# Moving a skipped overflow pass and the last weight loads around it, at the end of a two-layer mixture-of-experts kernel

## Chip, core and metric

The kernel runs on one core of a Trainium2 chip. The metric is device time in microseconds (us), the median of three runs of the whole kernel.

## The reference

Two layers on 256 latent and 256 context tokens of width 1024. Each has a mixer (a gated linear recurrence and pooling in layer 0, two kinds of attention in layer 1) and a mixture of experts: 4 groups of 8 experts, of which each token takes 2. In layer 1 only the latent tokens go on to the output, which is normalised. The part that the change touches is the mixture of experts of layer 1:

```python
def hier_moe(h, w_rg, b_rg, w_re, b_re, w_gate, w_up, w_down):
    ...
    comb = (g_p[:, :, None] * jax.nn.one_hot(g_idx[:, 0], MOE_GROUPS, dtype=jnp.float32)[:, :, None]
            * e_w[:, None, :]).astype(h.dtype)
    y = jnp.zeros_like(x)
    for g in range(MOE_GROUPS):
        a = jax.nn.silu(jnp.einsum('td,edf->tef', x, w_gate[g])) * jnp.einsum('td,edf->tef', x, w_up[g])
        y = y + jnp.einsum('tef,efd->td', a * comb[:, g, :, None], w_down[g])
    return y.reshape(b_, n, d)
...
    return rmsnorm(x, final_norm_g)
```

## The kernel before

The 32 experts of a layer are worked off in 8 quads of 4. Each expert has 32 slots (CAP), so a quad fills the 128 rows of a tile. For quad q the steps are, with the tiles that the profile names:

- `gather` picks the tokens of the quad with matmuls (xg) and evacuates them as X, 4 of 8 chunks on ACT and 4 on DVE.
- `gate_up` multiplies X by the gate and up weights (tiles g and u, 1 MB for each expert; 64 matmuls for each of the two), then makes sge.
- `turned` transposes sge to aT. `selection` builds the matrix sc that scatters the result: a broadcast matmul (bc) of rqT, the ranks of all tokens, which `rank_rows` makes with matmuls (rqT) and a cast on ACT.
- `down` multiplies aT by the down weights (tile d, 1 MB for each expert) to y, and `scatter` adds sc times z to x. For the last two quads the sums stay in PSUM (xo).

The steps of neighbouring quads overlap: in turn q of the loop in `moe` stand gate/up of q, scatter of q-2, down of q-1 and the gather for q+1. A scheduler orders the instructions of each engine when the program is built, except those that `keep` holds in program order.

Weights are loaded by SP, in the order of the program, into tiles from a ring of buffers (`wm`). Eight semaphores, DMAHW0 to DMAHW7, are used in turn, so that a load waits for the one eight before it. fg, the final gain (0.5 MB, one row spread over all partitions), is one such load.

An expert with more than 32 tokens is served by `overfull`: a branch on the largest count (`cmx`), and inside it loops over the quads that overflow. With these inputs the pass of layer 1 is skipped. Each engine loads the count into a register and branches for itself. The program of either side must leave the semaphores with the same counts: the not-taken side has, for each engine, waits until its own semaphores show all that was issued before, and adds what the pass would have added. For DMAHW0 to DMAHW7 SP does this, one after the other. `rank_rows` follows the branch, since the pass overwrites rqT.

Of the kernel before, what the change touches and what calls it, by code (L numbers as in the profile page):

```python
# [6 lines left out]
F32 = mybir.dt.float32  # L7
# [8 lines left out]
P = 128  # L16
D = 1024
# [55 lines left out]
def drain(*gens):  # L73
    for g in gens:
        for _ in g:
            pass
# [16 lines left out]
class K:  # L93
# [1312 lines left out]
    def moe(self, layer):  # L1406
        nc = self.nc
        V = nc.vector
        cap, nt, nq, S = self.CAP, self.nt, self.NQ4, self.S
        self.py = self.open(f"moey{layer}", side="right")  # L1410
        self.px = self.open(f"moex{layer}", side="right")
        self.p = p = self.open(f"moe{layer}", side="right")
        nr, nx, ny = self.RING, self.nx, self.YRING[layer]
        head = self.slots
        first = [(self.cst, "x0", 1)] + [(self.mla, f"s{i}", 1) for i in (1, 2, 0)] + [(self.yr, "yr", self.NYR)] * self.NYR if layer else []
        late = [(self.outer, "mh", 1), (self.outer, "ml", 1)] if layer else []
        rings = [[(self.ring, "w", nr)] * (nr - len(head)), [(self.xring, "xw", nx)] * nx]
        self.slots = head + first + rings[self.RO[layer]] + rings[1 - self.RO[layer]] + late + [(self.px if layer else self.py, "yw", ny - 1)] * (ny - 1) + [(self.px, "yl", 1)]
        self.prefetch(len(self.slots) - len(head) - 1)
        segs = list(range(S))  # L1420
        if layer:
            cmx = self.counts()
            drain(self.gather(self.rv, 0, 4, 0, self.X))
        if S > 1:
            self.gate2(0, 1, p, nc.gpsimd)

        def more(rv, q):
            self.rank_rows(rv)
            for s in segs:
                X = {}  # L1430
                if not layer:
                    self.over = self.px.tile([P, 2, 1024], F32, name="over", tag="yl")
                drain(self.gather(rv, 4 * q, 4, s, X, over=True))
                st = self.quad(q, X, [s], self.load_one)
                self.gate_up(st)
                self.turned(st)
                self.down(st, [s])
                self.scatter(st, [s])

        def overfull():  # L1440
            cnt = nc.values_load(cmx[0:1, nq:nq + 1], min_val=0, max_val=2 * P)
            with self.tc.If(cnt > cap):  # L1442
                rv2 = p.tile([P, nt, 32], F32, name="rv2")
                V.tensor_copy(rv2, self.rv)
                for q in range(nq):
                    es = slice(4 * q, 4 * q + 4)
                    cg = nc.values_load(cmx[0:1, q:q + 1], min_val=0, max_val=2 * P)
                    with self.tc.For_i(cap, cg, cap):
                        V.tensor_scalar_add(rv2[:, :, es], rv2[:, :, es], -float(cap))
                        more(rv2, q)  # L1450

        cur = self.quad(0, self.X, segs, self.load)
        if layer:
            self.gate_up(cur)
        else:
            self.low(0)
            self.gate_up(cur, 0, self.ranks)
            cmx = self.counts()
            drain(self.gather(self.rv, 0, 8, 1, self.X, low=self.low))
            overfull()  # L1460
            cur["X"] = dict(self.X)
            self.gate_up(cur, 1)
        self.prefetch(1)
        self.rank_rows(self.rv)
        Q = {}
        for q in range(nq):
            end = q == nq - 1
            if layer and end:
                self.scatter(Q[q - 2], segs)
                pre = {(key, 4 * q + j): self.load(key, 4 * q + j) for key in "gu" for j in range(4)}  # L1470
                Q[q - 1]["d"] = {j: self.load("d", 4 * q - 4 + j) for j in range(4)}
                dl = {j: self.load("d", 4 * q + j) for j in range(4)}
                self.pre.update(pre)
                self.fg = self.wm("fg")[:, :D]
                fg = self.I["final_norm_g"]
                nc.sync.dma_start(self.fg, bass.AP(tensor=fg.tensor, offset=fg.offset, ap=[[0, P], [1, D]]))
                self.over = self.xring.tile([P, 2, 1024], F32, name="over", tag="xw", bufs=self.nx)
                overfull()
                self.rank_rows(self.rv)
                self.keep = True  # L1480
                Q[q - 1]["into"] = True
            if cur is None:
                cur = self.quad(q, self.X, segs[::-1] if end else segs, self.load)
                self.gate_up(cur)
            if layer and end:
                cur["d"] = dl
            Q[q], cur = cur, None
            if S > 1 and q % 2 and not end:
                for s in segs:
                    drain(self.gather(self.rv, 4 * q + 4, 8, s, self.X))  # L1490
            if q > 1 and not (layer and end):
                self.scatter(Q[q - 2], segs)
            if layer and end:
                Q[q - 1]["py"] = {(0, hf): self.ps("y") for hf in range(2)}
                self.xo = {(n, hf): self.ps("xo") for hf in range(2) for n in range(2)}
                for n, hf in self.xo:
                    self.mmk(self.xo[n, hf], self.ident, self.xi(2 + n)[:, hf * 512:hf * 512 + 512], start=True, stop=False)
                self.selection(Q[q - 1])
            if q:
                self.down(Q[q - 1], segs)  # L1500
            self.turned(Q[q])
            if S == 1 and not end:
                drain(self.gather(self.rv, 4 * q + 4, 4, 0, self.X))
        self.scatter(Q[nq - 2], segs[::-1])
        for s in segs[::-1]:
            self.down(Q[nq - 1], [s])
            self.scatter(Q[nq - 1], [s])
        if layer:
            self.final()
        self.p.release()  # L1510
        self.px.release()
        self.py.release()
        self.mp.release()
        if layer:
            self.yr.release()
            self.outer.release()
            self.close_xring()
            self.mla.release()
# [9 lines left out]
    def load(self, key, e, *_):  # L1528
        return self.pre.pop((key, e), None) or self.fetch(self.wm(f"{key}_{self.layer}_{e}"), key, e)
# [234 lines left out]
    def down(self, st, segs):  # L1764
        nc, p, I = self.nc, self.p, self.I
        V, S, A = nc.vector, nc.scalar, nc.tensor
        q, parts, load, last = st["q"], st["parts"], st["load"], st["last"]
        py = st.get("py") or {(s, hf): self.ps("y") for s in segs for hf in range(2)}
        step = 1 if parts == 2 else 4
        kn = 2 // parts  # L1770
        for h in range(0, 4, step):
            for k0 in range(0, 2, kn):
                if parts == 2:
                    ws = {h: load("d", 4 * q + h, k0, k0 + kn)}
                else:
                    ws = st["d"] = st.get("d") or {j: load("d", 4 * q + j) for j in range(4)}
                for s in segs:
                    for hf in range(2):
                        for k in range(k0, k0 + kn):
                            for j, w in ws.items():  # L1780
                                r = slice(32 * j, 32 * j + 32)
                                first = not (h or k0 or hf or k or j or s != segs[0])
                                (self.mmy if parts == 1 and not self.layer and not first else self.mmk)(py[s, hf][r, :], st["aT"][s][:, k, r], w[:, k - k0, hf * 512:(hf + 1) * 512], start=k == 0, stop=k == 1)
        if last:
            zz = self.wm("z", F32R)
            self.yg = self.wm("yg")
# [61 lines left out]
```

## Time and profile before

| | |
|---|---|
| timed runs, median of 3 | 1088.25 us (1087.97 to 1088.27) |
| profiled execution, timed | 1088.17 us |
| its span in the profile | 1085.4 us |
| mean granted TensorE clock | 0.96 of full |
| busy: TensorE, VectorE, ScalarE, GpSimd | 89%, 49%, 37%, 22% of the span |
| read from HBM | 293.5 MB |

The span runs from the first to the last instruction of the profile; 2.8 us of the timed execution lie outside it. TensorE counts as busy from a matmul's start to its modelled end. PE is TensorE, PEld its weight loads, DVE is VectorE, ACT is ScalarE, POOL is GpSimd; a q behind a name is the engine's sequencer, which also waits, branches and issues DMAs. Line numbers are those of the kernel before; in the changed kernel the lines behind the edit in `moe` are 6 higher.

### The profile page before, as it was taken

The numbers are of one execution on the slowest core, as the hardware profiler recorded it, in microseconds if no ns is written. First come the engines' busy times: TensorE is split into PE (matmuls) and PEld (weight loads), VectorE is DVE, ScalarE is ACT, GpSimd is POOL, SyncE is SP. The second block draws the span as 40 slices with busy tenths as digits, with TensorE's granted clock in tenths as the row PEclk, the third lists the DMA queues.
The fourth block names the chain that finished last, engine by engine and source line by source line (L and its number), as shares of the span: only waits on it lengthen the run. The fifth ranks groups of instructions, "written<-read, shape, count | busy, mean of one in ns | idle before, by whom it ended". The sixth has DMA issues, their size and how long they took to land. (4 is left out here: it accounts for less than half of the span.)

```text
span 1085.4 us, 21427 instructions
## 1 busy us (share of the span) xinstructions
PE 963.8 (89%) x8935; PEld 612.2 (56%) x8935; DVE 530.8 (49%) x1134; ACT 396.8 (37%) x702; POOL 242.8 (22%) x258
## 2 busy tenths in 40 slices
PE   4999898968879789999999988999999799988876
PEld 2666575745657556575564536666666465543352
DVE  4439958595527833435354374234577623321213
ACT  4355455447645512121131136334665621100002
POOL 2216644543611400000000017544451100000000
PEclk9999999988989889999999999999999999999889
DMA  9974455462351449999989997853267779999994
GB/s 305 316 268 152 143 198 181 152 212 105 96 204 58 175 152 420 417 419 403 411 344 420 407 314 191 281 194 121 94 194 229 315 306 418 421 419 421 420 417 202
DMA packets 99315, 296.18 MB, mean 273 GB/s; under 512 B 23000, under 2 KB 57040, under 8 KB 74496
## 3 DMA queue, kind: packets, MB, share of 16 engines
q1 hardware_dynamic: 97344, 292.64, 71.4%
q8 instruction: 73, 1.20, 0.4%
q10 hardware_dynamic: 1200, 1.26, 0.4%
q0 software_dynamic: 656, 0.74, 0.2%
q14 instruction: 42, 0.34, 0.1%
HBM read 293.50 MB, written 1.11 MB: 271 GB/s over the span
## 5 line engine op out<-in xcount | busy, mean ns | idle before, releaser
L1705 PE MATMUL gu<-g,X 128*32 128x256 f32 x1536 | 103.0, 397 | 10.7 <-DVEq L1442 6.2
L1705 PE MATMUL gu<-u,X 128*32 128x256 f32 x1536 | 101.9, 394 | 11.6 <-DMA u<-in_moe_w_up_dram 11.6
L1758 POOL COPY esel<-idb 32x128 bf16<-32x128 bf16 x16 | 4.8, 299 | 435.5 <-PE bc L1738 305.7
L1711 ACT ACTIVATE sge<-gu 128x256 f32<-128x256 f32 x24 | 9.2, 384 | 213.5 <-PE gu L1705 213.5
L1705 PEld LDWEIGHTS gu<-u,X 128*32 128x32 f32 x1536 | 58.5, 113 | 48.4 <-DMA u<-in_moe_w_up_dram 15.1
L1705 PEld LDWEIGHTS gu<-g,X 128*32 128x32 f32 x1536 | 57.0, 114 | 49.5 <-issue 19.7
L1712 DVE SCALAR_TENSOR_TENSOR sge<-gu,ws,sge 128x256 f32<-128x256 f32 x24 | 11.6, 483 | 134.3 <-ACT sge L1711 134.3
L1818 DVE TENSOR_TENSOR x<-sc,x 128x512 f32<-128x512 f32 x88 | 56.6, 685 | 31.1 <-PE sc L1738 31.0
L1660 PE MATMUL xg<-onehot,h2h 128*128 128x128 f32 (+1 forms) x384 | 68.3, 294 | 2.4 <-DVE onehot L1648 1.4
L180 PE MATMUL pt<-hh,wh 128*128 128x512 f32 (+1 forms) x160 | 60.9, 380 | 4.1 <-ACT wh L173 3.6
L1666 DVE TENSOR_SCALAR X<-xg,ab 128x128 f32<-128x128 f32 (+1 forms) x60 | 27.8, 472 | 71.8 <-PE xg L1660 43.7
L182 PE MATMUL pt<-hh,wl 128*128 128x512 f32 (+1 forms) x160 | 59.2, 370 | 4.1 <-DVE wl L176 2.8
L1660 PEld LDWEIGHTS xg<-onehot,h2h 128*128 128x128 f32 x384 | 56.6, 200 | 10.8 <-issue 7.5
L1738 PE MATMUL sc<-z,sc 128*128 128x512 f32 x176 | 58.3, 465 | 2.5 <-ACT z L173 1.4
L1738 PE MATMUL y<-d,aT 128*32 128x512 f32 x274 | 60.3, 597 | 0.1
L181 PE MATMUL pt<-hl,wh 128*128 128x512 f32 (+1 forms) x160 | 57.7, 360 | 0.4 <-DVE hl L432 0.4
L1741 PE MATMUL y<-d,aT 128*32 128x512 f32 x494 | 58.0, 594 | 0.0
L176 POOL TENSOR_TENSOR wl<-wcol,wh 128x512 fp32r<-128x512 f32 (+1 forms) x32 | 43.2, 1353 | 59.6 <-ACT wh L173 53.1
L1664 ACT ACTIVATE X<-xg,ab 128x256 f32<-128x256 f32 (+1 forms) x68 | 34.1, 515 | 55.6 <-PE xg L1660 38.9
L173 ACT CAST z<-yg 128x512 fp32r<-128x512 f32 x34 | 21.0, 618 | 73.6 <-DVE yg L1797 73.6
L1738 PEld LDWEIGHTS sc<-z,sc 128*128 128x128 f32 x176 | 30.8, 188 | 29.2 <-issue 18.4
L181 PE MATMUL ptok<-wl,hh 128*128 128x512 f32 x96 | 40.9, 426 | 4.4 <-DVE wl L176 4.4
(402 smaller groups left out, 2044.1 us busy)
## 6 DMA issues: line engine op xcount, KB each, us to landing
g<-in_moe_w_gate_dram SPq DMA_DIRECT2D x64, 1024.0 KB, 15.5
u<-in_moe_w_up_dram SPq DMA_DIRECT2D x64, 1024.0 KB, 13.0
d<-in_moe_w_down_dram SPq DMA_DIRECT2D x64, 1024.0 KB, 12.7
wada<-in_ada_w_dram SPq DMA_DIRECT2D x48, 1024.0 KB, 6.7
wcol<-in_ab_w_in_dram SPq DMA_DIRECT2D x8, 1024.0 KB, 8.4
wcol<-in_cd_w_in_dram SPq DMA_DIRECT2D x5, 1024.0 KB
wtok<-in_ab_w_in_dram SPq DMA_DIRECT2D x4, 1024.0 KB, 5.5
wout<-in_ab_w_out_dram SPq DMA_DIRECT2D x4, 1024.0 KB, 8.1
```

Of the source, the lines that this page charges most:

```text
L173: nc.scalar.copy(hi, src)
L176: (el or nc.vector).tensor_tensor(lo, src, hi.bitcast(F32), op=ALU.subtract)
L180: mm(out, lh, rh, start=start, stop=False, **kw)
L181: mm(out, lh, rl, start=False, stop=False, **kw)
L182: mm(out, ll, rh, start=False, stop=stop, **kw)
L1660: nc.tensor.matmul(o, h, r, start=i == 0 and n_ == 0, stop=i == 1 and n_ == len(hs) - 1)
L1664: self.xk[k] = nc.scalar.activation(X[:, k], o, AF.Identity, scale=a2[:, k:k + 1], bias=b2[:, k:k + 1])
L1666: nc.vector.tensor_scalar(X[:, k], o, a2[:, k:k + 1], b2[:, k:k + 1], op0=ALU.mult, op1=ALU.add)
L1705: self.mm = A.matmul(pg[s][32 * j:32 * j + 32, c0:c0 + 256], X[:, k, x0 + 32 * j:x0 + 32 * j + 32], w[:, k - k0, :], start=k == 0 and c0 = ...
L1738: return self.kept(self.nc.tensor.matmul(*a, **kw))
L1741: return self.tc.keep_in_program_order(self.nc.tensor.matmul(*a, **kw))
L1818: nc.vector.tensor_tensor(self.xi(i)[:, cs], o, self.xi(i)[:, cs], op=ALU.add)
```

## The change

In the last turn of the loop (quad 7) stood, ahead of gate/up: the loads of g, u and d for the last two quads, fg, the overflow branch and `rank_rows`. They go to the turn of quad 6, behind its gate/up and scatter. The four down tiles of quad 7 are loaded in eight halves of 0.5 MB, first the rows k = 0 of all four, then k = 1, and `down` takes k as its outer loop for that quad. The tile `over`, which only the pass uses, comes from the ring `wm`. fg is issued by ACT behind the branch, no longer by SP ahead of it.

```diff
@@ -1467,16 +1467,6 @@
             end = q == nq - 1
             if layer and end:
                 self.scatter(Q[q - 2], segs)
-                pre = {(key, 4 * q + j): self.load(key, 4 * q + j) for key in "gu" for j in range(4)}
-                Q[q - 1]["d"] = {j: self.load("d", 4 * q - 4 + j) for j in range(4)}
-                dl = {j: self.load("d", 4 * q + j) for j in range(4)}
-                self.pre.update(pre)
-                self.fg = self.wm("fg")[:, :D]
-                fg = self.I["final_norm_g"]
-                nc.sync.dma_start(self.fg, bass.AP(tensor=fg.tensor, offset=fg.offset, ap=[[0, P], [1, D]]))
-                self.over = self.xring.tile([P, 2, 1024], F32, name="over", tag="xw", bufs=self.nx)
-                overfull()
-                self.rank_rows(self.rv)
                 self.keep = True
                 Q[q - 1]["into"] = True
             if cur is None:
@@ -1490,6 +1480,22 @@
                     drain(self.gather(self.rv, 4 * q + 4, 8, s, self.X))
             if q > 1 and not (layer and end):
                 self.scatter(Q[q - 2], segs)
+            if layer and q == nq - 2:
+                Q[q - 1]["d"] = {j: self.load("d", 4 * q - 4 + j) for j in range(4)}
+                pre = {(key, 4 * q + 4 + j): self.load(key, 4 * q + 4 + j) for key in "gu" for j in range(4)}
+                Q[q]["d"] = {j: self.load("d", 4 * q + j) for j in range(4)}
+                dl = {j: self.wm(f"d_1_{4 * q + 4 + j}").rearrange("p (k f) -> p k f", k=2) for j in range(4)}
+                for k in range(2):
+                    for j, t in dl.items():
+                        g, e = divmod(4 * q + 4 + j, 8)
+                        nc.sync.dma_start(t[:, k], self.I["moe_w_down"][1, g, e].rearrange("(p k) f -> p k f", k=2)[:, k])
+                self.pre.update(pre)
+                self.over = self.wm("over").rearrange("p (a b) -> p a b", a=2)
+                overfull()
+                self.rank_rows(self.rv)
+                self.fg = self.wm("fg")[:, :D]
+                fg = self.I["final_norm_g"]
+                nc.scalar.dma_start(self.fg, bass.AP(tensor=fg.tensor, offset=fg.offset, ap=[[0, P], [1, D]]))
             if layer and end:
                 Q[q - 1]["py"] = {(0, hf): self.ps("y") for hf in range(2)}
                 self.xo = {(n, hf): self.ps("xo") for hf in range(2) for n in range(2)}
@@ -1775,12 +1781,12 @@
                 else:
                     ws = st["d"] = st.get("d") or {j: load("d", 4 * q + j) for j in range(4)}
                 for s in segs:
-                    for hf in range(2):
-                        for k in range(k0, k0 + kn):
-                            for j, w in ws.items():
-                                r = slice(32 * j, 32 * j + 32)
-                                first = not (h or k0 or hf or k or j or s != segs[0])
-                                (self.mmy if parts == 1 and not self.layer and not first else self.mmk)(py[s, hf][r, :], st["aT"][s][:, k, r], w[:, k - k0, hf * 512:(hf + 1) * 512], start=k == 0, stop=k == 1)
+                    steps = [(hf, k) for hf in range(2) for k in range(k0, k0 + kn)]
+                    for hf, k in sorted(steps, key=lambda t: t[1]) if last else steps:
+                        for j, w in ws.items():
+                            r = slice(32 * j, 32 * j + 32)
+                            first = not (h or k0 or hf or k or j or s != segs[0])
+                            (self.mmy if parts == 1 and not self.layer and not first else self.mmk)(py[s, hf][r, :], st["aT"][s][:, k, r], w[:, k - k0, hf * 512:(hf + 1) * 512], start=k == 0, stop=k == 1)
```

How the instructions stand in the built programs, engine by engine, with the semaphores that each waits for (a number behind a name, as d_28, is the expert's; the last number is the buffer's):

SP before: its last loads, the branch, the end of the not-taken side (the row with all of DMAHW0 to DMAHW7) and the two output DMAs; the rows left out are those of the pass itself.

```order
L1525 DMA d_31_13276<-in_moe_w_down_dram 128x2048 [waits DMAHW2_49,PE_49]
L1476 DMA fg<-in_final_norm_g_dram 128x1024 [waits DMAHW3_49,PE_49]
L1442 COMPARE_AND_BRANCH
...
L1442 UNCONDITIONAL_BRANCH [waits SP_sequencer_49,DMAHW0_49,DMAHW1_49,DMAHW2_49,DMAHW3_49,DMAHW4_49,DMAHW5_49,DMAHW6_49,DMAHW7_49]
L1241 DMA out_dram<-yo 128x512 [waits DMAHW4_49,DVE_49]
L1241 DMA out_dram<-yo 128x512 [waits DMAHW5_49,DVE_49]
```

SP after, the same place.

```order
L1531 DMA d_27_13178<-in_moe_w_down_dram 128x2048 [waits DMAHW6_49,PE_49]
L1491 DMA d_28_13180<-in_moe_w_down_dram 128x1024 [waits DMAHW7_49,PE_49]
L1491 DMA d_28_13180<-in_moe_w_down_dram 128x1024 [waits DMAHW0_49]
L1491 DMA d_29_13181<-in_moe_w_down_dram 128x1024 [waits DMAHW1_49,PE_49]
L1491 DMA d_30_13182<-in_moe_w_down_dram 128x1024 [waits DMAHW2_49,PE_49]
L1491 DMA d_31_13183<-in_moe_w_down_dram 128x1024 [waits DMAHW3_49,PE_49]
L1442 COMPARE_AND_BRANCH
...
L1442 UNCONDITIONAL_BRANCH [waits SP_sequencer_49,DMAHW0_49,DMAHW1_49,DMAHW2_49,DMAHW3_49,DMAHW4_49,DMAHW5_49,DMAHW6_49,DMAHW7_49]
L1491 DMA d_29_13181<-in_moe_w_down_dram 128x1024 [waits DMAHW5_49]
L1491 DMA d_30_13182<-in_moe_w_down_dram 128x1024 [waits DMAHW6_49]
L1491 DMA d_31_13183<-in_moe_w_down_dram 128x1024 [waits DMAHW7_49]
```

fg has left SP, and the second halves of d_29, d_30 and d_31 have come to stand behind the branch.

ACT before, from the end of the not-taken side on.

```order
L1442 UNCONDITIONAL_BRANCH [waits Activation_49,Activation_sequencer_49]
L1632 CAST rqT<-rqT 32x256 [waits PE_49,Activation_49]
L1711 ACTIVATE sge<-gu 128x256 [waits DVE_49,PE_49]
L1752 COPY aT<-aT 128x256 [waits PE_49]
L358 ACT_TABLE_LOAD
```

ACT after, from the same place on.

```order
L1442 UNCONDITIONAL_BRANCH [waits Activation_49,Activation_sequencer_49]
L1498 DMA fg<-in_final_norm_g_dram 128x1024 [waits DMAHW1_49,DMAHW3_49,DVE_49,DMAHW4_49,PE_49,DMAHW6_49,Activation_49,Pool_49]
L1638 CAST rqT<-rqT 32x256 [waits PE_49]
L1670 ACTIVATE X<-xg,ab 128x128 [waits PE_49] x4
L1758 COPY aT<-aT 128x256 [waits PE_49]
L1717 ACTIVATE sge<-gu 128x256 [waits PE_49]
```

The load of fg stands first behind the branch, and behind it the cast and the four X of the last gather, which stood ahead of the branch before.

PE after, from the end of the not-taken side on (before, the last gate/up stood here).

```order
L1756 MATMUL aT<-ident,sge 128x128
L1636 LDWEIGHTS rq [waits DVE_49]
...
L1666 MATMUL xg<-onehot,h2h 128x128 [waits PE_49]
L1666 MATMUL xg<-onehot,h2h 128x128 x3
L1744 MATMUL y<-d_22_13152,aT 32x512 [waits DMAHW1_49]
L1744 MATMUL y<-d_22_13152,aT 32x512
L1744 LDWEIGHTS esel [waits Pool_49]
L1744 MATMUL bc<-rqT,esel 128x256 [waits Activation_49]
L1666 MATMUL xg<-onehot,h2h 128x128 [waits DVE_49]
```

The down of quad 5, its bc and the last gather have come behind the branch; bc waits for ACT, between the two halves of the gather.

## Rows read from the trace of the kernel before

**Rows 1.** The page's head: span and instructions.
```profile
span 1085.4 us, 21427 instructions
```

**Rows 2.** Windows: from:to, length, busy time of five engines (instructions), granted clock, DMA share, GB/s.
```profile
1040.00:1050.00 10.00, 3.83 (x30) 2.53 (x32) 1.75 (x4) 0.36 (x1) 0.28 (x1) 0.81 1.02 416
...
1070.00:1086.00 16.00, 5.56 (x35) 2.25 (x27) 7.17 (x21) 4.29 (x12) 0.00 (x0) 0.83 0.18 68
```

**Rows 3.** Timeline of SP: start, length (us), issues.
```profile
1032.40 17.70 SPq L1525 DMA_DIRECT2D d<-in_moe_w_down_dram  x8
...
1052.26 0.33 SPq L1476 DMA_DIRECT2D fg<-in_final_norm_g_dram  x1
```

**Rows 4.** DMA issues from 880 us on: count, KB each, median us to landing.
```profile
d<-in_moe_w_down_dram SPq DMA_DIRECT2D x28, 1024.0 KB, 19.8
```

**Rows 5.** The branch's line: duration in ns (min/median/max), first and last start.
```profile
L1442 SPq EVENT_SEMAPHORE  x9: 17/17/17, 1057.8 to 1071.1; - x9
...
L1442 ACTq EVENT_SEMAPHORE  x2: 17/17/17, 1043.2 to 1043.3; - x2
...
L1442 DVEq EVENT_SEMAPHORE  x2: 21/21/21, 1047.1 to 1047.2; - x2
...
L1442 ACTq COMPARE_BRANCH  x1: 45/45/45, 1038.0 to 1038.0; - x1
...
L1442 DVEq COMPARE_BRANCH  x1: 63/63/63, 1041.6 to 1041.6; - x1
...
L1442 SPq COMPARE_BRANCH  x1: 53/53/53, 1052.6 to 1052.6; - x1
```

**Rows 6.** SP's waits from 1020 us on: us in total, times, longest.
```profile
SPq L1442 <- SPq L1442: 18.2, 5, 6.8
...
SPq L1525 <- DMA d<-in_moe_w_down_dram: 8.4, 4, 2.1
```

**Rows 7.** Timeline: start, length, engine, count, [idle before <- what ended it].
```profile
1010.30 3.44 PE L1705 MATMUL gu<-g,X 128*32 128x256 f32 x59
...
1026.92 0.48 DVE L1712 SCALAR_TENSOR_TENSOR sge<-gu,ws,sge 128x256 f32<-128x256 f32 x1 [15.43 <-ACT sge L1711]
...
1032.22 1.60 PE L1660 MATMUL xg<-onehot,h2h 128*128 128x128 f32 x12
...
1037.45 3.70 PE L1738 MATMUL sc<-z,sc 128*128 128x512 f32 x8
...
1047.33 1.34 PE L1705 MATMUL gu<-g,X 128*32 128x256 f32 x8 [6.17 <-DVEq L1442]
...
1053.64 3.76 PE L1705 MATMUL gu<-u,X 128*32 128x256 f32 x64
...
1060.96 0.28 PE L1738 MATMUL bc<-rqT,esel 32*128 32x256 bf16 x1
...
1061.17 3.64 PE L1738 MATMUL y<-d,aT 128*32 128x512 f32 x32
...
1068.61 4.63 PE L1738 MATMUL y<-d,aT 128*32 128x512 f32 x32
...
1069.62 0.16 PEld L1738 LDWEIGHTS y<-d,aT 128*32 128x32 f32 x8 [0.86 <-SPq L1442]
```

**Rows 8.** Windows of 2 us behind the branch; columns as in rows 2.
```profile
1050.00:1052.00 2.00, 2.00 (x24) 2.00 (x20) 0.00 (x0) 0.00 (x0) 0.00 (x0) 0.50 0.98 401
...
1054.00:1056.00 2.00, 2.00 (x44) 2.00 (x39) 0.00 (x0) 0.00 (x0) 0.00 (x0) 1.00 1.00 418
```

**Rows 9.** Timeline of ACT.
```profile
1033.86 0.46 ACT L1664 ACTIVATE X<-xg,ab 128x128 f32<-128x128 f32 x1 [0.43 <-PE xg L1660]
...
1048.67 0.36 ACT L1632 CAST rqT<-rqT 32x256 bf16<-32x256 f32 x1 [10.68 <-PE rqT L1630]
...
1081.71 1.01 ACTq L1241 DMA_DIRECT2D out_dram<-yo  x2
```

**Rows 10.** Windows of 1 us; columns as in rows 2.
```profile
1070.00:1071.00 1.00, 1.00 (x16) 0.32 (x12) 0.00 (x0) 0.00 (x0) 0.00 (x0) 1.00 0.07 29
```

## The prediction

> **What bounds the kernel now.** I read the page's head first: the profiled execution spans 1085.4 us [rows 1] and was timed at 1088.17 us, so 2.8 us lie outside the span; the median of the three timed runs, 1088.25 us, is the same within 0.1 us. Everything the diff touches lies in the last 60 us, so I went to the windows of that stretch. The DMA engines are full (share 1.02, 416 GB/s, between 1040 and 1050 us) and nearly empty in the last 16 us, where 68 GB/s are left [rows 2]. The reader is to see a stream of weights that has no gap, with a short tail of compute behind it.
>
> SP's timeline says how that stream is fed: the last eight down tiles of 1 MB go out between 1032.4 and 1050.1 us, fg at 1052.26 us [rows 3], and a load lands 19.8 us after its issue [rows 4]. Eight loads are always under way, since the ninth waits for the first. TensorE is close behind. After the overflow branch it restarts at 1047.33 us, having stood still for 6.17 us, and runs almost without a break; its only later wait is 0.86 us at 1069.62 us, for the last down tile [rows 7]. So stream and TensorE end together: neither alone is worth more than about a microsecond, and whatever holds either of them by more than that goes straight into the time.
>
> **What the branch costs each engine.** In [rows 5] the view of line 1442 shows compare-and-branch at 1038.0 us on ACT, 1041.6 on DVE and 1052.6 on SP, and the first semaphore event of the not-taken side at 1043.2, 1047.1 and 1057.8: 5.2 to 5.5 us from one to the other on each engine. They cross independently; TensorE went on at 1047.3, 5 us before SP came to the branch. SP is the exception in what it does there. On the not-taken side it waits for every load in front of the branch before it adds the counts of the pass. That is the 18.2 us in five waits [rows 6], from 1052.6 to its last event at 1071.1 us, when fg has landed; the DMA engines move 29 GB/s in the microsecond up to there [rows 10]. Before the change only the two output DMAs stand behind this wait in SP's order, and their data come later still.
>
> **The change, part by part.**
>
> *The branch itself.* It is crossed once in either kernel, so its 6.17 us on TensorE move and do not go: from the front of the last gate/up to the end of the last-but-one. DVE's last work there ends at 1027.4 us (0.48 us after 1026.92 [rows 7]), so with 5.5 us the engines are past it at about 1033. Taken alone: 0.
>
> *The loads in front of it.* The order of the loads stays, so the stream up to d27 is the same. But the built program has only five of the eight half loads in front of the branch; the second halves of d29, d30 and d31 stand behind SP's not-taken wait. In front of it lie 3 x 0.5 MB less than before, and fg's 0.5 MB.
>
> *fg on ACT.* This decides. ACT's first instruction after the branch is the fg load, with waits on DMAHW3 and DMAHW4 among others. In the built program the value awaited on DMAHW3 is 1856; the loads in front of the branch bring it to 1472, and the 384 between are what SP adds on its not-taken side. So ACT cannot issue fg before SP has seen its loads land. ACT runs in order: behind fg stand the cast of rqT, the four X evacuations of the last gather, and aT. TensorE's broadcast matmul (bc) needs the cast, and all of the last quad is behind bc.
>
> The Trainium skill ("DMA: Bandwidth & Descriptors", section "Issuing engines are not separate DMA queues") says that starting DMAs from several engines saves only the sequencer's time to start them; by that alone the move of fg is worth SP's 0.33 us and no more, which is rival A. The same page ("Anatomy of one DMA — SWDGE (gpsimd) path") says that a semaphore wait is served on the issuing sequencer before dispatch, and that speaks against this change. The trace agrees for SP: its sequencer stands for 2.1 us ahead of a load until an earlier one has landed, 8.4 us in four times [rows 6]. No row before shows ACT so held; rival A is the case that it isn't.
>
> *When SP lets go (T0).* d31's first half is issued where fg was, at 1052.26 us, when d24 lands. Check the method on before: then d25 to d31 and fg are to come, 7 x 1.049 + 0.524 = 7.86 MB, at the stream's 0.418 MB/us [rows 8] 18.8 us, so 1071.1, which is what SP shows. After: d25 to d27, and five halves, 3.15 + 2.62 = 5.77 MB, 13.8 us: T0 = 1066.1 us.
>
> *From T0 on.* ACT issues fg (two DMA issues of ACT end 1.01 us after the first began, so 0.5) and casts rqT (0.36) [rows 9]; with 0.1 for the handing over, bc runs at 1067.1. By then TensorE has done the first half of the gather and has stood for about 29 us.
> - Rest of gather 7, down of quad 5, scatter of quad 5: before, the same stretch runs from 1032.22 to 1041.15 (from the xg x12 of 1.60 us to the end of the sc x8), 8.9 us at full clock [rows 7]. The new order leaves 16 xg matmuls of the trace, not 12 (+0.5), and bc (0.28 in the same rows): 9.7.
> - The clock: after the 6.17 us stall the granted clock is 0.50 (1.2 GHz) and back at 1.00 (2.4 GHz) some 6 us after the restart [rows 8]. I take the same 6 us at half clock after the longer wait: +3.0. So the scatter ends at 1079.8.
> - Last gate/up: its tiles have long landed and the clock is up. 64 g matmuls at the pace of 59 in 3.44 us are 3.7, 64 u matmuls 3.76 [rows 7]: 7.4, to 1087.2. (Before, at the low clock, it took 10.07.)
> - What follows took 1085.4 - 1057.4 = 28.0 before. The wait for d31 goes: y x32 took 4.63 us there and 3.64 for the quad before [rows 7], so 27.0.
>
> End of span 1114.2, plus 2.8: **1117.0 us**.
>
> *The row halves* cost and gain nothing in this sum. The three late halves and fg are 2.1 MB, 5.0 us at the stream's pace; with 2 us for the slow end of a stream (an estimate from the 29 GB/s of its last microsecond [rows 10]) they have landed by 1074, and are read past 1098. What hides them is the last quad's work; without it they would be the wait of rival A. Order k outside hf lets the first half of y end 0.9 us later relative to the second and lets both yg products follow at once; bounds -0.9 and +0.9, taken as 0.
>
> *Unknown costs.* T0: from 1065.8 (d31's landing at 1069.6 less 1.57 MB) to 1068, if loads of 4 KB rows go at the tail's lower pace. Clock: 0 (up at once) to +5 us (nearly all of the 9.7 us at half clock); the value taken is that of the nearest row. ACT after release: its X evacuations are 0.46 us each [rows 9]; if PE finds fewer chunks done, 0 to +1.5.
>
> **Rivals.**
> A. *ACT is not held*: fg's waits are met without SP. Then TensorE does the same work as before, in another order, and the end is set by the three halves that SP issues after its own wait: T0 1066.1, 1.57 MB at 0.418 is 3.8, about 2 to land (the estimate above), so 1072; the last two of four groups of y (half of 3.64 us) end at 1073.8 where before they ended at 1073.2. Time 1088.9, no change. For it: no row of before shows ACT held at a load. Against: the not-taken side is the only place that can bring that count to 1856. It decides if ACT's rqT cast comes before 1040.
> B. *The change does what it says*: all halves effectively in time, the branch hidden under the wait for the u tiles. Then the 0.86 us wait goes, and the last landing is followed by half of y, not all: with d31 at 1069.6, y ends at 1071.3, not 1073.2. Time 1086.3. Against: the order has three halves behind the branch, and SP's 18.2 us show what they wait for. It decides if the last half lands before 1070.
> C. *The restart is worse*: the clock stays down through the last gate/up too, as it did before over the g half; 9.7 + 7.4 us at half clock cost 17.1, not 3.0: 1131.
>
> **How the numbers follow.** Forecast 0.91; A 0.05; B 0.02; C 0.02. With every low bound (T0 -0.3, clock -3, y -0.9) the sum is 1112.8; with every high one (+1.9, +5, +1.5, +0.9) 1126.3, which would need four mishaps at once, and two of them make 1121 to 1122. I give 1112 to 1122 us; it leaves out A, B, C and that corner, together about 0.15. A measurement of this kernel tells about 0.2% (2.2 us) from no change: A and most of B are within it. Slower by over 0.2%: 0.92; within: 0.06; faster: 0.02.
>
> **What would show it.** Right: ACT idle from about 1032 to 1066.5 ahead of its rqT cast; SP's not-taken wait ending near 1066, with three 0.5 MB loads right behind it; TensorE idle for about 29 us ahead of bc, granted clock 0.5 for some 6 us from there; last gate/up of about 7.4 us; no wait in the last y. Wrong: a cast of rqT before 1050 (A), or T0 far from 1066, which would mean that the loads in front of the branch are gated by something other than the stream.

## The result, and the profile after

The changed kernel takes 1118.17 us in the median of four runs (1114.35 to 1120.73); the kernel before took 1088.21 beside it (1087.97 to 1088.27). The ratio is 1.0268, interval 1.0244 to 1.0293: 29 to 30 us slower. The profiled execution took 1120.51 us, and its span is the page's head:

```profile
span 1118.6 us, 21430 instructions
```

SP's timeline (columns as in [rows 3]) shows the loads of the last quads. Eight half loads stand in one row, which lasts 25.31 us where the eight whole ones lasted 17.70:

```profile
1027.98 7.79 SPq L1531 DMA_DIRECT2D u<-in_moe_w_up_dram  x4
1037.92 7.78 SPq L1531 DMA_DIRECT2D d<-in_moe_w_down_dram  x4
1047.86 25.31 SPq L1491 DMA_DIRECT2D d<-in_moe_w_down_dram  x8
```

Before, the four u loads began at 1022.46 us. The whole stream was 5.5 us later in this execution, already ahead of everything that the change touches; more on that below.

The branch's line (columns as in [rows 5]) says when each engine crossed and when SP was through:

```profile
L1442 SPq EVENT_SEMAPHORE  x9: 17/17/17, 1063.4 to 1071.8; - x9
...
L1442 ACTq EVENT_SEMAPHORE  x2: 17/17/17, 1036.4 to 1036.5; - x2
L1442 DVEq EVENT_SEMAPHORE  x2: 21/21/21, 1037.4 to 1037.5; - x2
...
L1442 ACTq COMPARE_BRANCH  x1: 45/45/45, 1031.4 to 1031.4; - x1
L1442 DVEq COMPARE_BRANCH  x1: 63/63/63, 1031.8 to 1031.8; - x1
L1442 SPq COMPARE_BRANCH  x1: 53/53/53, 1058.2 to 1058.2; - x1
```

ACT was across at 1036.5, yet its timeline has nothing until SP's last event at 1071.8. Then, within a tenth of a microsecond, fg is issued, and the cast of rqT follows; in brackets stands how long ACT was idle, and that SP's line of the branch ended it:

```profile
1071.80 0.39 ACTq L1498 DMA_DIRECT2D fg<-in_final_norm_g_dram  x1
1072.23 0.36 ACT L1638 CAST rqT<-rqT 32x256 bf16<-32x256 f32 x1 [40.83 <-SPq L1442]
```

TensorE's timeline shows the branch at the end of quad 6's gate/up, then some work, and then the wait for that cast. From bc on it runs through to the end of the last y, with no wait in it (the 0.86 us of [rows 7] are gone):

```profile
1037.65 3.63 PE L1744 MATMUL y<-d,aT 128*32 128x512 f32 x8 [6.68 <-DVEq L1442]
...
1044.49 1.90 PE L1744 MATMUL y<-d,aT 128*32 128x512 f32 x4
1072.64 0.37 PE L1744 MATMUL bc<-rqT,esel 32*128 32x256 bf16 x1 [26.25 <-ACT rqT L1638]
1072.94 3.78 PE L1666 MATMUL xg<-onehot,h2h 128*128 128x128 f32 x16
...
1080.48 3.70 PE L1744 MATMUL sc<-z,sc 128*128 128x512 f32 x8
1084.11 3.66 PE L1711 MATMUL gu<-g,X 128*32 128x256 f32 x64
1087.59 3.64 PE L1711 MATMUL gu<-u,X 128*32 128x256 f32 x64
1091.15 3.70 PE L1744 MATMUL xo<-x,ident 128*128 128x512 f32 x8
...
1102.44 3.64 PE L1744 MATMUL y<-d,aT 128*32 128x512 f32 x32
1106.01 0.28 PE L1744 MATMUL bc<-rqT,esel 32*128 32x256 bf16 x1
```

The windows (columns as in [rows 2]) show what the wait does to the clock and to the stream. The granted clock is at the lower level, 0.50, through the wait and for some 5 us behind the restart; the DMA engines run nearly dry in the two microseconds ahead of SP's release and then carry only the late halves and fg:

```profile
1060.00:1070.00 10.00, 0.00 (x0) 0.00 (x0) 0.00 (x0) 0.00 (x0) 0.00 (x0) 0.50 0.93 377
1070.00:1072.00 2.00, 0.00 (x0) 0.00 (x0) 0.00 (x0) 0.00 (x0) 0.00 (x0) 0.50 0.15 61
...
1074.00:1076.00 2.00, 2.00 (x11) 2.00 (x11) 0.51 (x2) 0.46 (x1) 0.00 (x0) 0.50 0.91 254
1076.00:1078.00 2.00, 2.00 (x16) 0.89 (x18) 0.31 (x1) 0.46 (x1) 0.00 (x0) 0.74 0.94 340
1078.00:1080.00 2.00, 2.00 (x24) 0.64 (x17) 0.69 (x1) 0.00 (x0) 0.00 (x0) 1.00 0.79 322
```

So the time went where the forecast put it: from the last weights' landing, which ended the kernel before, to one wait of TensorE in front of bc.

### The profile page after: what moved, and what is told of

Its sections match the earlier page's. It is cut to its first block, busy times and chain, and to the rows that moved or that the text cites. A ratio compares the mean times of both kernels' runs of the same rounds, so it can differ in the third digit from the quotient of the medians.

```text
span 1118.6 us, 21430 instructions
## 1 busy us (share of the span) xinstructions
PE 971.7 (87%) x8935; PEld 614.0 (55%) x8935; DVE 531.1 (47%) x1134; ACT 396.3 (35%) x702; POOL 242.4 (22%) x258
## 5 line engine op out<-in xcount | busy, mean ns | idle before, releaser
L1711 PE MATMUL gu<-g,X 128*32 128x256 f32 x1536 | 99.5, 389 | 4.3 <-DVE rq L1633 4.3
L1666 PEld LDWEIGHTS xg<-onehot,h2h 128*128 128x128 f32 x384 | 61.3, 216 | 36.7 <-issue 33.4
L1711 PEld LDWEIGHTS gu<-g,X 128*32 128x32 f32 x1536 | 53.1, 112 | 43.6 <-issue 12.6
L1666 PE MATMUL xg<-onehot,h2h 128*128 128x128 f32 (+1 forms) x384 | 73.2, 311 | 2.4 <-DVE onehot L1654 1.4
L1672 DVE TENSOR_SCALAR X<-xg,ab 128x128 f32<-128x128 f32 (+1 forms) x60 | 27.8, 471 | 76.7 <-PE xg L1666 48.6
```

Of the source, the lines that this page charges most:

```text
L1666: nc.tensor.matmul(o, h, r, start=i == 0 and n_ == 0, stop=i == 1 and n_ == len(hs) - 1)
L1672: nc.vector.tensor_scalar(X[:, k], o, a2[:, k:k + 1], b2[:, k:k + 1], op0=ALU.mult, op1=ALU.add)
L1711: self.mm = A.matmul(pg[s][32 * j:32 * j + 32, c0:c0 + 256], X[:, k, x0 + 32 * j:x0 + 32 * j + 32], w[:, k - k0, :], start=k == 0 and c0 = ...
```

## The experiments

The theory, H: ACT stands at the fg load until SP's not-taken side is through, and all that stands behind fg in ACT's order stands with it. The rivals: the place of the branch costs the time (R); the row halves do; any load issued by ACT does.

Single times scatter by several microseconds; in the profiles the stream of layer 1's weights starts earlier or later from one execution to the next. So each run is read in two ways: by its ratio to the kernel before (interval in brackets), and, in its profile, by its **tail**: the span less the first issue of the last quad's u loads in SP's timeline. For the kernel before the tail is 1085.4 - 1022.46 = 62.9 us, for the changed one 1118.6 - 1027.98 = 90.6, a difference of 27.7. A tail comes from one execution, and it differs from the ratio's difference by up to 3.5 us (e9: 12.0 beside 8.5), so smaller differences between two tails say little by themselves. Below, runs are named by the first part of their label.

| run | fg issued by | down tiles | ratio to before | tail, us (and less 62.9) |
|---|---|---|---|---|
| changed kernel | ACT, first behind the branch | halves | 1.0268 [1.0244, 1.0293] | 90.6 (+27.7) |
| e1_fg_sp | SP, behind the branch | halves | 1.0036 [1.0018, 1.0054] | 69.7 (+6.8) |
| e3_branch_only | SP, behind the branch | whole | 0.9998 [0.9980, 1.0016] | 63.0 (+0.1) |
| e5_whole_fgact | ACT, first behind the branch | whole | 1.0272 [1.0249, 1.0294] | 94.7 (+31.8) |
| e11_fg_act_late | ACT, behind its last aT | whole | 1.0001 [0.9982, 1.0020] | 62.9 (0.0) |
| e7_fg_pool | GpSimd, first behind the branch | halves | 1.0259 [1.0228, 1.0291] | 90.7 (+27.8) |
| e8_last_half | SP, behind the branch | d31 alone in halves | 1.0030 [1.0008, 1.0052] | 66.3 (+3.4) |
| e9_nobranch | ACT, no branch | halves | 1.0078 [1.0048, 1.0108] | 74.9 (+12.0) |
| e10_nobranch_fgsp | SP, no branch | halves | 0.9986 [0.9970, 1.0002] | 62.2 (-0.7) |
| e2_fg_act (kernel before) | ACT, first behind the branch | whole | 1.0105 [1.0076, 1.0134] | 73.5 (+10.6) |
| e4_halves (kernel before) | SP, ahead of the branch | halves | 0.9989 [0.9971, 1.0007] | 61.8 (-1.1) |

### Take fg off ACT

```diff
-                nc.scalar.dma_start(self.fg, ...)
+                nc.sync.dma_start(self.fg, ...)
```

> The changed kernel, but fg is issued by SP behind the branch, not by ACT; nothing else differs. Theory H (ACT stands at fg until SP's not-taken side is through, and everything behind rqT's cast stands with it): the cast of rqT comes before 1045 us, no wait of TensorE is longer than 8 us, and what is left is the landing of the three late halves: T0 about 1066, landing 1072, time 1088.9 us (1087 to 1091). If the stream of loads runs 5.5 us late ahead of the change, as it did in the profiled execution of the changed kernel, 5.5 us more (1094). Rival R (the place of the branch and the order of the last two quads cost the time, and fg's engine is harmless): 1113 us or more.

Measured: 1093.5 us in the median of 12, before 1088.76 beside it. 25 of the 29 us are gone with one word, and R falls. ACT's cast came at 1042.59 us, behind its matmuls and not behind SP, in a stream as late as that of the changed kernel (1028.47):

```profile
1042.59 0.36 ACT L1638 CAST rqT<-rqT 32x256 bf16<-32x256 f32 x1 [10.97 <-PE rqT L1636]
```

But the run is 3.9 us slower than before (0.36% of 1089), where H said 1088.9, no change. TensorE's timeline shows the rest, two waits in the last y for late halves:

```profile
1074.24 2.98 PE L1744 MATMUL y<-d,aT 128*32 128x512 f32 x20
1077.83 1.05 PE L1744 MATMUL y<-d,aT 128*32 128x512 f32 x2 [0.60 <-DMA d<-in_moe_w_down_dram]
1081.37 3.62 PE L1744 MATMUL y<-d,aT 128*32 128x512 f32 x10 [2.50 <-DMA d<-in_moe_w_down_dram]
```

The chain of the work that ended last (start, length, what) goes through the last of the three halves: it is issued at 1073.22 and takes 8.11 us to land, 9.0 from SP's release at 1072.3. Behind that wait the granted clock is 0.50: the ten last matmuls took 3.62 us, where the same ten take 1.90 in e8 at a granted clock of 1.00.

```profile
1073.22 8.11 DMA d<-in_moe_w_down_dram
```

### Take the halves away too, and move the branch alone

To the edit above comes:

```diff
-                dl = {j: self.wm(f"d_1_{4 * q + 4 + j}").rearrange("p (k f) -> p k f", k=2) for j in range(4)}
-                for k in range(2):
...
+                dl = {j: self.load("d", 4 * q + 4 + j) for j in range(4)}
...
-                    for hf, k in sorted(steps, key=lambda t: t[1]) if last else steps:
+                    for hf, k in steps:
```

> The changed kernel with whole down tiles of the last quad in their old order of use, and fg issued by SP behind the branch: what is left of the change is the place of the branch and of rank_rows, and the loads in front of it. H: all down tiles are in front of the branch; ACT is not held; d31 lands at 1069.6 as before and all of the last y stands behind it: 1088.2 us (1086.5 to 1090), 5.5 more if the stream runs late ahead of the change. R: 1113 or more.

Measured: 1088.32 us in the median of 12, ratio 0.9998. The move of the branch, with all loads and `rank_rows`, is worth nothing that these runs can tell; the interval leaves room for 2 us either way.

### Whole tiles, fg still on ACT

The edit is the second one alone.

> The changed kernel with whole down tiles of the last quad in their old order of use; fg stays on ACT behind the branch. H: SP's not-taken side now waits for all four down tiles, so it lets go when d31 has landed, 1069.8 us, 3.7 later than the 1066.1 of the five halves; from there 0.8 to bc, 11.5 to the end of quad 5's scatter, 7.1 for the last gate/up, 27.4 to the end, 2.8 outside: 1119.5 us (1117 to 1122), 5.5 more if the stream runs late. The halves thus make the hold shorter. R (row halves and order k outside hf are part of the cost): earlier than the changed kernel, below 1112.

Measured: 1118.48 us (4 runs, 1117.58 to 1119.38), with the stream where it was before (1022.30). SP let go at 1069.8, as said, and ACT went on there:

```profile
1069.81 0.35 ACTq L1494 DMA_DIRECT2D fg<-in_final_norm_g_dram  x1
1070.20 0.36 ACT L1634 CAST rqT<-rqT 32x256 bf16<-32x256 f32 x1 [43.60 <-SPq L1442]
```

Counted from the first issue of the u loads, the release came after 47.5 us here (1069.8 - 1022.30) and after 43.8 in the changed kernel (1071.8 - 1027.98), a difference of 3.7: three halves, 1.57 MB, are 3.8 us at the 0.418 MB/us of [rows 8]. The tail is 4.1 us longer. So the halves didn't cause the loss; in the profiles, three of them behind the branch made the hold shorter. The ratios (1.0272 and 1.0268) don't show that difference.

### fg on ACT, in the kernel before

```diff
-                self.fg = self.wm("fg")[:, :D]
...
-                nc.sync.dma_start(self.fg, ...)
                 self.over = self.xring.tile(...)
                 overfull()
+                self.fg = self.wm("fg")[:, :D]
...
+                nc.scalar.dma_start(self.fg, ...)
                 self.rank_rows(self.rv)
```

> The kernel before, but fg is issued by ACT behind the branch; branch, loads and order stay where they were. H: SP's not-taken side ends when d31 has landed, at about 1069.8 us (no fg in front); until then ACT casts no rqT and makes no sge of the last gate/up. TensorE ends that gate/up at about 1057.4 and then stands for some 13 us; from the release 0.5 (fg), 0.4 (cast), then the 27 us that follow the last gate/up in the changed kernel, up to 3 for the clock, 2.8 outside the span: 1104 us (1101 to 1108). R: 1088.2, as before, since the order is that of before.

Measured: 1098.44 us, +11.4 by the ratio. With the branch left where it was, the one moved load holds ACT in the same way:

```profile
1068.45 0.35 ACTq L1478 DMA_DIRECT2D fg<-in_final_norm_g_dram  x1
1068.90 0.36 ACT L1632 CAST rqT<-rqT 32x256 bf16<-32x256 f32 x1 [33.25 <-SPq L1442]
```

TensorE waits in front of bc again, 11.3 us here:

```profile
1069.31 0.37 PE L1738 MATMUL bc<-rqT,esel 32*128 32x256 bf16 x1 [11.34 <-ACT rqT L1632]
```

The mechanism held and the size didn't: 1104 was expected. The release came as said (the stream was 1.4 us earlier than before), but I had counted 27 us behind it, and TensorE had done the 3.7 us of xo<-x,ident during the wait; the clock cost less than the 3 us as well (y took 5.36 us, 1.7 more than at full clock).

### fg on GpSimd

```diff
-                nc.scalar.dma_start(self.fg, ...)
+                nc.gpsimd.dma_start(self.fg, ...)
```

> The changed kernel, but fg is issued by GpSimd behind the branch. H (whichever engine has fg in its order behind the branch stands until SP's not-taken side is through): GpSimd stands at fg, and behind it the copy esel for quad 5, which bc needs; so TensorE waits in the same place and as long, only on esel now: 1118 us (1114 to 1121), with ACT's rqT cast before 1045. Rival P (GpSimd has a queue of its own and is not held): as with fg on SP, 1093.5 (1091 to 1097).

Measured: 1117.28 us (4 runs), ratio 1.0259. ACT cast rqT at 1035.22 and was free; now GpSimd stood, and TensorE waited in front of the same bc, for esel. The line of the branch for SP, and GpSimd's and TensorE's timelines:

```profile
L1442 SPq EVENT_SEMAPHORE  x9: 17/17/17, 1056.6 to 1065.0; - x9
```

```profile
1065.48 0.57 POOL L1498 DMA_DIRECT2D fg<-in_final_norm_g_dram  x1 [134.90 <-SPq L1442]
1066.06 0.30 POOL L1764 COPY esel<-idb 32x128 bf16<-32x128 bf16 x1
```

```profile
1066.41 0.39 PE L1744 MATMUL bc<-rqT,esel 32*128 32x256 bf16 x1 [27.29 <-POOL esel L1764]
```

Its tail is that of the changed kernel within 0.1 us. So ACT and GpSimd make no difference as the issuer here; what counts is that bc needs something that stands behind the load. Of the 134.9 us, GpSimd would have been idle for most in any case: in e1 it stands 98.0 us ahead of the same copy.

### fg on ACT, but later in its order

The kernel of the third experiment, with fg issued behind ACT's last aT copy:

```diff
-                nc.scalar.dma_start(self.fg, ...)
...
             self.turned(Q[q])
+            if layer and end:
+                with self.tc.issue_after(self.aTi.ins):
+                    nc.scalar.dma_start(self.fg, ...)
```

> The changed kernel with whole down tiles of the last quad in their old order of use, and fg issued by ACT, but behind ACT's last aT copy instead of first behind the branch. H (not the issuer counts but what stands behind the load in its order): ACT makes rqT, X, sge and aT unhindered, stands at fg from about 1065.5 to SP's release at 1069.8, and only the table load and work that is needed later is behind it: as with fg on SP, 1 us less to 1.5 us more than the kernel before. Rival (a load on ACT behind the branch costs the time wherever it stands): 1110 or more.

Measured: ratio 1.0001. ACT does stand at fg, from the end of aT at 1067.42 to SP's last event at 1071.9, and nobody waits for it:

```profile
1067.05 0.37 ACT L1756 COPY aT<-aT 128x256 f32<-128x256 f32 x1 [7.49 <-PE aT L1754]
1071.91 0.35 ACTq L1505 DMA_DIRECT2D fg<-in_final_norm_g_dram  x1
```

### Leave the branch out

The branch of layer 1 is left out, and with it the overflow pass; in the second of the two runs fg is on SP as well.

```diff
-                overfull()
```

> The changed kernel without the overflow branch of layer 1: the branch and the pass it skips are left out; fg stays on ACT, in front of the X of the last gather, and the eight halves follow one another. H (it is SP's not-taken side that holds ACT, not ACT as the issuer): ACT waits at fg only for the load before it on its semaphore, u31, which lands at about 1050; TensorE reaches the last gate/up about then, and the end is set by the stream: 1088 us (1085 to 1091). Rival L (any load on ACT is held until the stream's last loads have landed, branch or no branch): 1110 or more.

Measured: 1099.13 us, ratio 1.0078. H was right about the release and wrong about the time (1088 was expected), and L was wrong in both. ACT was released when u31 had landed, at 1051.0, as expected of H, and not with the end of the stream:

```profile
1051.01 0.34 ACTq L1497 DMA_DIRECT2D fg<-in_final_norm_g_dram  x1
1051.47 0.81 ACT L1669 ACTIVATE X<-xg,ab 128x128 f32<-128x128 f32 x2 [25.00 <-DMA u<-in_moe_w_up_dram]
```

```profile
1051.98 2.93 PE L1665 MATMUL xg<-onehot,h2h 128*128 128x128 f32 x12 [19.53 <-ACT X L1669]
```

What I had missed is what stands behind it: xg waits for X, and most of quad 5's down and its scatter stand behind xg in TensorE's order. It lost 19.5 us there and came back at the low clock. So the ordinary wait of a load for the one eight before it, which SP shows all the time ([rows 6], 2.1 us), costs 8.5 us by the ratio when ACT has to do the waiting (about 10 beside e10 below, which differs in fg's issuer alone); SP's not-taken side makes of that the 29.

> The changed kernel without the overflow branch of layer 1 (branch and pass left out) and with fg issued by SP behind the eight halves: no engine is held. H (the stream of loads sets the end, and the branch as such costs next to nothing): last half at 1069.6, 5 of the 16 groups of y behind it (1.1 us, 2.2 at the low clock), where before y ended 3.6 behind: 1.3 to 2.5 us less than the kernel before, so 1086 where that takes 1088.2. This bounds what any place of the branch can bring. Rival (the branch's 6.2 us of TensorE lie on the path): 5 us less or more.

Measured: ratio 0.9986, 1.5 us less, which the interval doesn't quite tell from nothing. No engine is held, TensorE waits in the last gate/up for the u tiles instead of the branch (3.9 us in three waits), and the stream ends the kernel where it did. So with these loads no place of the branch can be expected to bring more than this, 3.3 us at the low end of the interval.

### The halves by themselves

The kernel before, with the eight half loads and the k order of the change; all eight are ahead of the branch, then fg.

> The kernel before with the row halves alone: the four last down tiles in eight halves, k = 0 of all four first, and k as the outer loop of the last down; the branch stays where it was and fg is issued by SP in front of it, behind the halves. All eight halves are in front of the branch. H (halves do no harm as long as they are not behind the branch): y of the last quad needs only 5 of its 16 groups after the last half, so the 0.86 us wait goes: 1 us less than the kernel before, between 2 us less and no change. R (halves with rows of 4 KB take longer on the DMA engines): 1 us more or worse.

Measured: ratio 0.9989, 1.2 us less; the sign is what H said, the interval (0.9971 to 1.0007) includes no change. In front of the branch the halves do no harm. The reason in H holds in part only. The wait in the last y didn't go:

```profile
1068.79 4.64 PE L1742 MATMUL y<-d,aT 128*32 128x512 f32 x32
```

It takes 4.64 us (4.63 before), and its weight loads stand idle for 0.87 us ahead of the last half's, at 1071.53. What became shorter is the work behind it: y ended 1.9 us after the wait, where it ended 3.6 after it before. The 5 of 16 groups take 1.9 us, not the 1.1 (5/16 of 3.64) that I counted in e8 and e10.

Then the changed kernel with fg on SP and only d31 in halves, so that one half stands behind the branch:

```diff
+                dl = {j: self.load("d", 4 * q + 4 + j) for j in range(3)}
+                dl[3] = self.wm(f"d_1_{4 * q + 7}").rearrange("p (k f) -> p k f", k=2)
                 for k in range(2):
-                    for j, t in dl.items():
+                    for j, t in [(3, dl[3])]:
```

> The changed kernel with fg issued by SP behind the branch, d28 to d30 loaded whole and d31 alone in two halves. Now one half of 0.5 MB and fg stand behind the branch, where three halves and fg stood with all tiles in halves. H (what the run with fg on SP lost against the kernel before is the landing of the halves behind the branch, 8.1 us from the last one's issue with fg beside it): T0 1068.3, the half lands some 5 us later, 1073.5, and 5 of 16 groups of y follow, 1.1: 1.5 us more than before, up to 4 if the clock falls in the wait, so +1 to +4. Rival: the loss lies in the halves themselves or in their order of use, not in their place: as with all in halves, +4.7.

Measured: ratio 1.0030, 3.3 us more, within what H allowed. SP let go at 1069.2, and the half came into use 4.3 us later:

```profile
1068.88 2.77 PE L1745 MATMUL y<-d,aT 128*32 128x512 f32 x22
1073.47 1.90 PE L1745 MATMUL y<-d,aT 128*32 128x512 f32 x10 [1.82 <-DMA d<-in_moe_w_down_dram]
```

The interval overlaps that of three halves, so these two runs don't tell the number of halves apart; that the place does it is shown with the run before it, where eight halves ahead of the branch cost nothing.

## Why the prediction was right, step by step

- **"This decides" (fg on ACT): right.** e1 takes nearly all of the loss away by moving that load alone, e3 and e11 all of it with whole tiles; e2 brings 11 us of it back in the kernel before, and e7 all of it on another engine. The rule that the prediction set against the change, from the Trainium skill ("DMA: Bandwidth & Descriptors", section "Anatomy of one DMA — SWDGE (gpsimd) path"), that a semaphore wait is served on the issuing sequencer, holds here for ACT too (idle for 40.8 us, where e1 shows 11.0) and for GpSimd (134.9, where e1 shows 98.0). The other ("Issuing engines are not separate DMA queues"), that several issuers save only the time to start, agrees with the runs where nothing that is needed soon stands behind the load: 1.0001 in e11 beside 0.9998 in e3.
- **T0: right in method, 5.7 us late in time.** 5.5 of them are the lateness of the stream in this execution, which no term held; the term itself was short by 0.2. e7 has the same loads with a stream 1.3 us early (1021.16), and there SP's last event came at 1065.0, where the method gives 1064.8. So T0 far from 1066, named as a sign of being wrong, came about with the stream as the gate all the same.
- **From T0 on: right.** T0 to bc took 0.8 (forecast 1.0). bc to the end of the scatter took 11.5 (12.7): the work is 9.5 at full clock (1046.45 to 1055.99 in e1), so the clock cost 2.0, not 3.0; the same stretch took 11.0 in e7 and 12.3 in e5, so this cost varies between 1.5 and 2.8. The last gate/up took 7.0 (7.4), what follows 27.4 (27.0), and 1.9 us lay outside the span (2.8). The sum of the profiled run: 1117.0 + 5.7 - 0.2 - 1.2 - 0.4 + 0.4 - 0.9 = 1120.4, with 1120.51 measured. Without the late stream it would be 1115; the runs of 1114.35 and 1115.84 are near that, but they have no profile that shows where their stream was. That 1117.0 lies close to the median, 1118.17, is thus in part luck: in this execution the terms were about 2 us too long in sum, and the late stream, which no term held, added 5.5. TensorE's wait ahead of bc was 26.2 us, not about 29; nothing in the sum hangs on it.
- **The range's far corner was added up wrongly.** The clock's bound of +5 us is given as the whole cost, of which 3.0 is in the sum already, so with every high bound the time is 1123.3, not 1126.3. The words beside it, "nearly all of the 9.7 us at half clock", would by rival C's count be a cost of 9.7 and not 5. The measured cost, 1.5 to 2.8, stays far below either.
- **The branch itself, "0": right** (e3, 0.9998; left out altogether, 0.9986).
- **The row halves, "cost and gain nothing in this sum": right** under the hold, which covers their landing: no wait in the last y.
- **Rival A was priced wrong.** It said that without the hold the late halves would end at 1072 and the time would not change. e1 is that case, and it is slower by 0.36%. The step that failed is "1.57 MB at 0.418 is 3.8, about 2 to land": the last half landed 9.0 us after the release, not 5.8. The stream starts again from empty, runs at 311 to 336 GB/s in e1's windows of 2 us, and shares that with fg right behind; how the loss divides between the restart and fg wasn't tried. The low clock behind the wait made the end of y 1.7 us longer on top. The rival's condition was too simple as well: e9 shows that fg's waits hold ACT to 1051 even where SP's not-taken side is gone.
- **Rival B**, 1086.3 if all went as the change reads, was of the right size (e10, -1.5 us): even then the gain could hardly be told from nothing.
- **Rival C** (the clock stays down through the last gate/up) was wrong: full again some 5 us after the restart.

What stays open is why the stream starts at different times: 1021.1 to 1028.5 us in the twelve profiles, and the kernel before itself took 1085.91 to 1095.57 us in 23 runs beside e1. The traces of before and after part between 830 and 900 us, in layer 1's mixer, on instructions that the change leaves alone; the granted clock of the three windows of 20 us from 820 on is 0.95, 0.88 and 0.74 after, beside 1.00, 1.00 and 0.83 before. The cause wasn't tried.

## What to carry to other kernels

A load is not free for the engine that issues it: every semaphore that it waits for is waited for in that engine's order. Before a load is moved to another engine, read the value that it waits for, ask who brings that value and when, and list what stands behind it there; here one word of the change cost 25 us, and the same load a few instructions later in ACT's order cost nothing that twelve runs could tell. And a stream that sets the end of a kernel must not be cut by something that waits for all of it to land: what is issued behind such a wait pays the restart, here 8 to 9 us for three half loads that needed 3.8 at pace.

## What was unexpected of the hardware

- Crossing the skipped branch took these engines 5.0 to 5.6 us from compare to the first event of the other side with the DMA engines full (ACT 1031.4 to 1036.4, DVE 1031.8 to 1037.4, SP 1058.2 to 1063.4). At the same branch of layer 0, with 4 to 12 GB/s moving, it took 2.5 to 2.9 (ACT 387.1 to 389.9, DVE 388.4 to 391.3, SP 383.9 to 386.4). The Trainium skill ("Runtime: NRT & Kernel Launch", section "Instruction fetch mechanics") says that a taken branch whose target lies outside the two pages at hand makes the engine fetch it by DMA before it can go on. The two measurements agree with that, but no run here separates it from other causes.
- When the clock was back after a stand didn't follow the length of the stand. TensorE had stood 26 us in the changed kernel, 27 in e7, 30 in e5 and 11 in e2. In windows of 2 us, the granted clock was 1.00 for the first time in the one that began 5.4 us after the restart in the changed kernel, 3.6 in e7, 7.4 in e5 and 4.7 in e2; in the window before that one it was 0.74, 0.60, 0.85 and 0.72.
